# Gate/up weights: two of the seven low parts of a half step made by an accumulating DMA

## The chip, the cores and the metric

The kernel runs on one core of a Trainium2 chip. The metric is the device time of one execution in microseconds. Before the change two runs took 1078.86 and 1079.63 us; the median is 1079.24.

## What is computed

The reference is a decoder trunk of two layers on 512 tokens of width 1024, all in float32. Each layer is a mixer and a feed-forward part, each with an RMS norm before and after it and a residual sum. Layer 0 mixes with two kinds of attention, layer 1 with a causal pooling. The change touches the first half of the feed-forward part alone, the gate and up projections:

```
def swiglu(h, w_gate, w_up, w_down):
    return (jax.nn.silu(h @ w_gate) * (h @ w_up)) @ w_down
```

`w_gate` and `w_up` are 1024 x 2816, `w_down` is 2816 x 1024, one of each per layer.

## The kernel before

**Split operands.** TensorE multiplies float32 in a rounded form (the type fp32r in the rows). To keep the precision, every operand is kept as a high part (rounded to fp32r) and a low part (what the rounding left), and each product is three matmuls: high by high, high by low of the activations, and low by high (`three`, L325 to L328; L328 is the one that reads the weight's low part). For weights the parts are made by `conv` (L235 to L238): ScalarE copies the float32 operand into the fp32r tile `wh` (L237), and VectorE, for the gate/up weights, subtracts that copy from the operand into `wl` (L238; key `slo`). Each part is a tile of 128 x 512 float32, 256 KB.

**Half steps.** Gate and up are done by column pairs: 11 pairs of 2 x 128 columns per layer, for each pair first gate and then up, so 22 half steps per layer and 44 in all. A half step is one level of a Strassen-Winograd scheme with seven products of 256 columns, each 12 matmuls. Its weights are seven operands of four row blocks: '11', '22', 's1', 's3', '12', 's2', 's4', in the order in which `pair_weights` (L889 to L923) makes them. They come from two raw tiles `wr` of 512 KB, loaded by SP (L894); raw tile 0 holds blocks a11 and a12, raw tile 1 a21 and a22. The sums s1 to s4 are made in place in those tiles (`comb`, L904 to L906): s1 = a21 + a22 into a22 on VectorE, s3 = a11 - a21 into a21 on POOL, s2 = s1 - a11 into a11 on VectorE, s4 = a12 - s2 into a12 on POOL. So the 's4' sum overwrites a12, which is the operand of '12' before that, and it may only do so when both parts of '12' have been made from it.

**Short steps.** For three pairs of layer 0 and two of layer 1 the products with '11' and '12' are made ahead, while the norms of the layer are still running (`front`). Their half steps lack '11' and '12' and have five products. In each layer these pairs alternate with others until they are used up, so the first part of a gate/up stretch has full and short half steps in turn, and the rest has full ones alone.

**Products and banks.** `run` (L925 ff.) puts out, for half step i: `begin` with '11' (bank psA, operand uh) and '22' (psO, th), then `end` of step i-1 with 's4' (psS, uh), then `middle` with 's1' and 's3' (psS, th), '12' (psA, uh) and 's2' (psO, th). VectorE adds the products up from PSUM (L951 to L957 and L963), ScalarE does the silu (L967), POOL the product of gate and up (L977).

**Buffers and order.** All high and low parts of weights share ten tiles, the tag `wq`, five parts' worth; the raw tiles have four, the tag `wr`, two half steps' worth. A planner walks through the instructions with its own estimate of what each costs, takes for each engine the ready instruction of the highest priority, and fixes by that the order on every engine; `tc.high_priority` moves weight preparation to the front. On the chip each engine then runs its list in that order and waits at an instruction whose inputs or buffers are not ready. DMAs are issued by SP, a few by ScalarE, none by POOL.

Of the kernel before, what the change touches and what calls it, by code (L numbers as in the profile page):

```python
# [9 lines left out]
AF = mybir.ActivationFunctionType  # L10
ALU = mybir.AluOpType
AX = mybir.AxisListType

P = 128
# [15 lines left out]
CFG = dict(  # L30
    order=ORDER,
    norm='vggvgvvg',
    wlo0='g',
    wlo1='ggv',
    ng=31,
    no=8,
    xe=4,
    pt=4,
# [2 lines left out]
    jk=2,  # L41
    psb=(2, 2, 2, 2),
    early=('kc', 'vc'),
    hpe=50,
    hpw=0,
    wloe='g',
# [9 lines left out]
    slo='v',  # L56
# [56 lines left out]
def trunk(ctx: ExitStack, tc, x, norm_g, w_in, b_f, cmp_pe, cmp_w1, cmp_w2, w_out,  # L113
          pool_w, pool_scale, w_gate, w_up, w_down, cst_d, bands_d, out):
    nc = tc.nc
# [40 lines left out]
    def BANK(tag, shape=(P, S)):  # L156
        return ps.tile(list(shape), F32, tag=tag, bufs=psb[tag], name=nm(tag))

    def r32(ap):
        return ap.bitcast(F32)  # L160
# [4 lines left out]
    def cols(w, c0, n, k0=0, nk=KC):  # L165
        return w[k0 * P:(k0 + nk) * P, c0:c0 + n].rearrange("(k p) f -> p k f", p=P)

# [1 line left out]
    cst = cp.tile([P, C_END], F32, name="cst")  # L169
    ident = cst[:, C_ID:C_ID + P]  # L170
    strip_nsa = cst[:, C_NSA:C_NSA + S]
# [34 lines left out]
        nc.tensor.transpose(pp[:, 0:64], pe2, ident[0:64, 0:64])  # L206
        nc.scalar.activation(peTs, pp[:, 0:64], AF.Copy)

# [1 line left out]
    def split(dst_hi, dst_lo, src):  # L210
        nc.scalar.activation(dst_hi, src, AF.Copy)
        nc.vector.tensor_sub(dst_lo, src, r32(dst_hi))
# [7 lines left out]
    def load_w(src, shape, alloc=None):  # L220
        raw = T(shape, "wr", CFG["wr"])
        nc.sync.dma_start(raw, src)
        return split_w(raw, shape, alloc)
# [8 lines left out]
    def next_engine(key):  # L232
        return nc.vector if choose(key) == "v" else nc.gpsimd

    def conv(hi, lo, src, key="wlo"):  # L235
        with tc.high_priority(CFG["hpw"]):
            nc.scalar.activation(hi, src, AF.Copy)  # L237
            next_engine(key).tensor_tensor(lo, src, r32(hi), op=ALU.subtract)  # L238
# [59 lines left out]
        return T([P, KC, S], "uh", 1, F32R), T([P, KC, S], "ul", 1, F32R)  # L298

    def transpose_pair(dst, srcs, ks, tag, gcol=None):  # L300
        """dst(k) -> (hi, lo) of [128, 256]: the transposed column blocks ks of two token tiles"""
        pt = BANK(tag)
        for a, k in enumerate(ks):
            for j in range(2):
                nc.tensor.transpose(pt[:, a * 256 + j * P:a * 256 + (j + 1) * P], srcs[j][:, k * P:(k + 1) * P], ident)
        hi, lo = dst
        if gcol is None:
            split(hi, lo, pt.rearrange("p (k c) -> p k c", k=2))
            return
        for a, k in enumerate(ks):  # L310
            g = gT[:, gcol * 8 + k:gcol * 8 + k + 1]
            o = pt[:, a * 256:(a + 1) * 256]
            nc.scalar.activation(hi[:, a, :], o, AF.Copy, scale=g)
            nc.vector.scalar_tensor_tensor(lo[:, a, :], o, g, r32(hi[:, a, :]), op0=ALU.mult, op1=ALU.subtract)
# [20 lines left out]
            three(pa[:, 0:cs.stop - cs.start], wh[k], wl[k], uh[:, k, cs], ul[:, k, cs], k == 0, k == KC - 1)  # L335
        return pa

    # ================= layer 0: FoX || NSA =================
    w0 = w_in[0]
    early = [split_w(raw, [P, KC, P]) for raw in early_raw]  # L340
    u = alloc_u()
# [24 lines left out]

    env = {}

    # -- block compression --
    kcs = cp.tile([P, 2, 2, 32], F32R, name="kcs")  # L370
    kcA, kcB = kcs[:, :, 0, :], kcs[:, :, 1, :]
    nc.gpsimd.memset(r32(kcs), 0.0)
# [57 lines left out]
                        move(VCs[g][rows, r, 0:DH], tmp[0:NCB, g, DH:P])  # L430
                        move(VCs[g][rows, r, DH:P], tmp[0:NCB, g, 0:DH])

    # -- keys and queries, stacked along the contraction --
    def key_stack(name):
        pa = proj0(name)
        res = []
        with tc.high_priority(CFG["hpe"]):
            for g in range(2):
                q = slice(g * DH, (g + 1) * DH)
                o = slice((1 - g) * DH, (2 - g) * DH)  # L440
                kh, kl = (G([P, S], F32R, label=n_) for n_ in ("knh", "knl"))
                nc.scalar.activation(kh[q], pa[q, :], AF.Copy)
                nc.vector.tensor_sub(kl[q], pa[q, :], r32(kh[q]))
                move(kh[o], kh[q])
                move(kl[o], kl[q])
                res.append((kh, kl))
        return res
# [32 lines left out]
                    move(kB[DH + 2 + i:DH + 3 + i], env["cc"][i][h:h + 1])  # L480
                fx[h] = ((qA, kA), (qB[0:DH + 4], kB[0:DH + 4]))

    # -- values: [token, d] with high and low parts side by side --
    def v_load(pieces, groups, alloc):
        ws = []
        width = sum(n for _, n in pieces)
        k0 = 0
        for g_, nk in enumerate(groups):
            raw = T([P, nk, width], "wr", CFG["wr"])
            c = 0  # L490
            for c0, n in pieces:
                nc.sync.dma_start(raw[:, :, c:c + n], cols(w0, c0, n, k0, nk))
                c += n
            k0 += nk
            if alloc is None:
                his, los = split_w(raw, [P, nk, width])
            else:
                hi, lo = (alloc(g_, [P, nk, width], l_) for l_ in ("vwh", "vwl"))
                conv(hi, lo, raw)
                his, los = ([w_[:, k, :] for k in range(nk)] for w_ in (hi, lo))  # L500
            ws += list(zip(his, los))
        return ws
# [14 lines left out]
                with tc.high_priority(CFG["hpe"]):  # L517
                    put(per * tp + j, pa[:, j * width:(j + 1) * width])

    # -- forget gates and branch gates, projected beside the values of the NSA branches --  # L520
    def nsa_values():
        gt = cp.tile([P, NT, 32], F32, name="gates")

# [24 lines left out]
        nc.vector.scalar_tensor_tensor(cc[1], c, 8.0, r32(cc[0]), op0=ALU.mult, op1=ALU.subtract)  # L548
        env["gt"], env["cc"] = gt, cc

    # -- softmax and P^T for one (head, branch) and half of the queries --
    def softmax_unit(half, passes, strip, scale, gate):
        E = XE([P, 1024], label="E")
        its = (0, 1) if half == 0 else (2, 3)
# [209 lines left out]
            res.append(t_)  # L764
        return res

    # -- out[token, :] = sum over contraction chunks; the last chunks token tile by token tile --
    def down(get, nchunk, w, res):
        banks, acts = {}, {}

# [57 lines left out]
    class Ffn:  # L828
# [6 lines left out]
            self.g = bcast(norm_g[layer, 2], "g2", where)  # L835

        def weights(self, p):
            """the first column chunk of a pair, whose two products with the first half of the tokens run ahead"""
            self.ws[p] = [load_w(cols(w_[self.layer], 2 * p * P, P), [P, KC, P], pair_g if p < CFG["eg"] else None)
                          for w_ in (w_gate, w_up)]  # L840

# [20 lines left out]
            next_engine("mul").tensor_tensor(a[0][:, 0:256], a[0][:, 0:256], a[1][:, 0:256], op=ALU.mult)  # L862

        def combine(self):
            """T1 = B12 - B11, T2 = B22 - T1, T3 = B22 - B12, T4 = B21 - T2, each transposed and split"""
            lo_, hi_ = slice(0, S), slice(S, D)
            ts = [[], [], [], []]
            for j in range(2):
                a, b = self.uns[j], self.uns[2 + j]
                t1, t2, t3, t4 = (G([P, S], label="tt") for _ in range(4))  # L870
                for o, x0, x1 in ((t1, b[:, lo_], a[:, lo_]), (t3, b[:, hi_], b[:, lo_]),
                                  (t2, b[:, hi_], t1), (t4, a[:, hi_], t2)):
                    next_engine("sadd").tensor_tensor(o, x0, x1, op=ALU.subtract)
                for m, t_ in enumerate((t1, t2, t3, t4)):
                    ts[m].append(t_)
            self.T = {}
            for n_, m in enumerate((0, 2, 3, 1)):
                his, los = [], []
                for k2 in range(2):
                    hi, lo = (G([P, 2, 256], F32R, label=l_) for l_ in ("th", "tl"))  # L880
                    transpose_pair((hi, lo), ts[m], (2 * k2, 2 * k2 + 1), "psT")
                    his += [hi[:, k, :] for k in range(2)]
                    los += [lo[:, k, :] for k in range(2)]
                self.T[m + 1] = (his, los)
# [2 lines left out]
            return [[u_[:, 4 * j + k, t * 256:(t + 1) * 256] for k in range(4)] for u_ in self.u]  # L887

        def pair_weights(self, w_, p):  # L889
            """the blocks of two column chunks and the sums of a Strassen-Winograd step, high and low parts"""  # L890
            raws = []
            for a in range(2):
                raw = T([P, KC, P], "wr", CFG["wr"])
                nc.sync.dma_start(raw, cols(w_, (2 * p + a) * P, P))  # L894
                raws.append(raw)
            (a11, a12), (a21, a22) = ((r_[:, 0:4, :], r_[:, 4:8, :]) for r_ in raws)
            W = {}

            def put(name, src):
                hi, lo = WQ2([P, 4, P])  # L900
                conv(hi, lo, src, "slo")
                W[name] = ([hi[:, k, :] for k in range(4)], [lo[:, k, :] for k in range(4)])

            def comb(o, x0, x1, op):  # L904
                with tc.high_priority(CFG["hpw"]):
                    next_engine("sadd").tensor_tensor(o, x0, x1, op=op)  # L906

            if p not in self.ws:
                put("11", a11)
            put("22", a22)  # L910
            comb(a22, a21, a22, ALU.add)
            put("s1", a22)
            comb(a21, a11, a21, ALU.subtract)
            put("s3", a21)
            if p not in self.ws:
                put("12", a12)
            comb(a11, a22, a11, ALU.subtract)
            put("s2", a11)
            comb(a12, a12, a11, ALU.subtract)
            put("s4", a12)  # L920
            return W
# [127 lines left out]
    for step in CFG["tr1"].split():  # L1049
        steps[step[0]](*(int(c) for c in step[1:]))  # L1050

    # ================= layer 1: pooling mixer =================
    class Pool:
        def __init__(self):
            self.v = []
# [130 lines left out]
```

## Time and profile before

| | |
|---|---|
| two runs, median | 1078.86 and 1079.63 us, 1079.24 us |
| profiled execution: span, first to last instruction | 1076.4 us |
| the two runs above that span | 2.5 and 3.2 us |
| mean granted TensorE clock | 0.987 |
| gate/up of layer 0 | about 320 to 548 us |
| gate/up of layer 1 | about 720 to 950 us |

The profiled execution has no time of its own beside the span; the runs lie 2.5 to 3.2 us above it. A share of busy time on the page is a mean over the whole span, in which the stretches differ much; a group's mean duration covers the instruction alone and beside other engines; and the end of a matmul is modelled, so the distance from one matmul's start to the next says more than its length. A row's bracket names the idle time of the engine ahead of the instruction and who ended it.

### The profile page before, as it was taken

Reading aid. Unit: us, or ns where it says so; the run is one execution under the profiler, and the core shown is the slowest. Engines: PE = TensorE matmul, PEld = TensorE weight load, DVE = VectorE, ACT = ScalarE, POOL = GpSimd, SP = SyncE. Lnnn points to the kernel's source line nnn. Section 1 sums busy time; section 2 is a strip of 40 time slices with the busy share of each in tenths; the row PEclk is TensorE's granted clock in tenths of the full one; section 3 lists DMA queues with packets and bytes.
Section 4 is the critical chain, followed back from the end, with each engine's and each line's share of the span. In section 5 each row is a group of like instructions: output and inputs, shape, how many; then the busy total and the mean of one; then the engine's idle time right before and its main releaser. Section 6 shows DMA issues by size and latency. Waiting matters only on the chain.

```text
span 1076.4 us, 18708 instructions
## 1 busy us (share of the span) xinstructions
PE 1032.2 (96%) x6892; PEld 944.7 (88%) x6892; DVE 783.5 (73%) x1488; ACT 563.5 (52%) x1172; POOL 511.0 (47%) x421
## 2 busy tenths in 40 slices
PE   7999999999999999999999998989999999999997
PEld 6899888977899989899988886989889999988886
DVE  4449797767578999999991034788999999992123
ACT  5557797688465344444472234664444444472221
POOL 3815667666762444434454353362444334454340
PEclk9999999999999999999999999799999999999999
DMA  7920202233603333333334355003343343334222
GB/s 226 205 62 21 79 12 70 61 115 121 177 22 97 112 107 109 105 113 98 104 113 132 118 159 154 21 11 90 97 118 101 96 118 99 99 118 137 88 69 79
DMA packets 153419, 108.55 MB, mean 101 GB/s; under 512 B 11764, under 2 KB 134512, under 8 KB 153328
## 3 DMA queue, kind: packets, MB, share of 16 engines
q1 hardware_dynamic: 152528, 106.22, 33.7%
q8 instruction: 54, 0.88, 0.3%
q10 hardware_dynamic: 800, 1.15, 0.3%
q14 instruction: 37, 0.30, 0.1%
HBM read 101.88 MB, written 2.10 MB: 97 GB/s over the span
## 4 chain that ended last, share of the span: by engine, by line
PE 73%; DVE 15%; ACT 4%; issue 4%; DMA 2%; POOL 2%; DVEq 0%; POOLq 0%; ACTq 0%; SPq 0%
PE psA L328 5%; PE psA L326 5%; PE psA L327 5%; DVE wl L238 5%; PE psS L326 5%; PE psS L328 5%; PE psS L327 5%; PE psO L326 3%; PE psO L327 3%; PE psO L328 3%; PE psT L774 2%; PE psT L775 2%; PE psO L775 2%; PE psT L776 2%; PE psO L774 2%
## 5 line engine op out<-in xcount | busy, mean ns | idle before, releaser
L237 ACT ACTIVATE wh<-wr 128x512 fp32r<-128x512 f32 x420 | 252.8, 626 | 314.2 <-DVE wr L906 106.9
L238 DVE TENSOR_TENSOR wl<-wr,wh 128x512 fp32r<-128x512 f32 x318 | 297.0, 959 | 106.0 <-ACT wh L237 105.3
L238 POOL TENSOR_TENSOR wl<-wr,wh 128x512 fp32r<-128x512 f32 x102 | 144.4, 1426 | 137.7 <-ACT wh L237 128.6
L328 PE MATMUL psA<-uh,wl 128*128 128x256 f32 (+1 forms) x408 | 129.3, 317 | 0.5 <-DVE wl L238 0.5
L326 PE MATMUL psA<-uh,wh 128*128 128x256 f32 (+1 forms) x408 | 128.7, 315 | 0.4 <-ACT comb L940 0.4
L327 PE MATMUL psA<-ul,wh 128*128 128x256 f32 (+1 forms) x408 | 128.1, 314 | 0.0
L906 POOL TENSOR_TENSOR wr<-wr,wr 128x512 f32<-128x512 f32 x44 | 57.4, 1304 | 142.0 <-DVE wr L906 97.6
L906 POOL TENSOR_TENSOR wr<-wr 128x512 f32<-128x512 f32 x44 | 59.3, 1348 | 105.9 <-DVE wl L238 80.1
L326 PE MATMUL psS<-th,wh 128*128 128x256 f32 x352 | 100.9, 287 | 6.6 <-ACT wh L237 4.8
L328 PE MATMUL psS<-th,wl 128*128 128x256 f32 x352 | 101.4, 288 | 4.5 <-DVE wl L238 4.3
L327 PE MATMUL psS<-tl,wh 128*128 128x256 f32 x352 | 100.5, 286 | 0.0
L328 PE MATMUL psO<-th,wl 128*128 128x256 f32 x352 | 99.8, 284 | 0.6 <-DVE wl L238 0.6
L327 PE MATMUL psO<-tl,wh 128*128 128x256 f32 x352 | 99.8, 284 | 0.0
L326 PE MATMUL psO<-th,wh 128*128 128x256 f32 x352 | 99.5, 284 | 0.0
L328 PEld LDWEIGHTS psA<-uh,wl 128*128 128x128 f32 x408 | 78.3, 192 | 6.9 <-DVE wl L238 2.8
L326 PEld LDWEIGHTS psA<-uh,wh 128*128 128x128 f32 x408 | 78.2, 192 | 4.6 <-ACT comb L940 0.6
L327 PEld LDWEIGHTS psA<-ul,wh 128*128 128x128 f32 x408 | 78.3, 192 | 3.8
L977 POOL TENSOR_TENSOR act<-comb,comb 128x512 f32<-128x512 f32 (+1 forms) x44 | 71.9, 1649 | 11.6 <-DVE comb L963 6.2
L326 PEld LDWEIGHTS psS<-th,wh 128*128 128x128 f32 x352 | 67.7, 192 | 8.0 <-ACT wh L237 5.8
L328 PEld LDWEIGHTS psS<-th,wl 128*128 128x128 f32 x352 | 67.8, 193 | 6.8 <-DVE wl L238 6.7
L264 POOL TENSOR_SCALAR E<-E,ri 128x128 f32<-128x128 f32 (+3 forms) x48 | 54.6, 1139 | 40.0 <-DVE ri L582 16.7
L328 PEld LDWEIGHTS psO<-th,wl 128*128 128x128 f32 x352 | 67.4, 192 | 1.5 <-DVE wl L238 1.5
(343 smaller groups left out, 2972.2 us busy)
## 6 DMA issues: line engine op xcount, KB each, us to landing
wr<-in_ffn_w_gate_dram SPq DMA_DIRECT2D x49, 512.0 KB
wr<-in_ffn_w_up_dram SPq DMA_DIRECT2D x49, 512.0 KB
wr<-in_ffn_w_down_dram SPq DMA_DIRECT2D x44, 512.0 KB
wr<-in_attn_w_in_dram SPq DMA_DIRECT2D x20, 512.0 KB
wr<-in_attn_w_out_dram SPq DMA_DIRECT2D x8, 512.0 KB
x<-in_x_dram SPq DMA_DIRECT2D x4, 512.0 KB
gbc<-in_norm_g_dram SPq DMA_DIRECT2D x8, 256.0 KB
h<-in_x_dram SPq DMA_DIRECT2D x4, 512.0 KB
```

The source lines that it names most:

```text
L237: nc.scalar.activation(hi, src, AF.Copy)
L238: next_engine(key).tensor_tensor(lo, src, r32(hi), op=ALU.subtract)
L264: (nc.vector if k == "v" else nc.gpsimd).tensor_scalar(e, e, s1, None, op0=ALU.mult)
L326: nc.tensor.matmul(psum, wh, ah, start=first, stop=False)
L327: nc.tensor.matmul(psum, wh, al, start=False, stop=False)
L328: nc.tensor.matmul(psum, wl, ah, start=False, stop=last)
L774: nc.tensor.matmul(o, acts[c][0][:, tok], wh[k], start=first, stop=False)
L775: nc.tensor.matmul(o, acts[c][0][:, tok], wl[k], start=False, stop=False)
L776: nc.tensor.matmul(o, acts[c][1][:, tok], wh[k], start=False, stop=last)
L906: next_engine("sadd").tensor_tensor(o, x0, x1, op=op)
L977: next_engine("mul").tensor_tensor(a_, xg[:, rows, :], xu[:, rows, :], op=ALU.mult)
```

## The change

The low parts of '12' and 's4' are no longer made by ScalarE and a VectorE subtraction, but by ScalarE twice and a DMA that POOL issues: ScalarE writes the negated operand, rounded to fp32r, into the low tile, then the operand, rounded, into the high tile; then the DMA reads the float32 operand from the raw tile and adds it onto the low tile, which so holds operand minus high part. The other five parts are made as before. 

```
+    dlo=('12', 's4'),
...
             def put(name, src):
                 hi, lo = WQ2([P, 4, P])
-                conv(hi, lo, src, "slo")
+                if name in CFG["dlo"]:
+                    with tc.high_priority(CFG["hpw"]):
+                        nc.scalar.activation(lo, src, AF.Copy, scale=-1.0)
+                        nc.scalar.activation(hi, src, AF.Copy)
+                        nc.gpsimd.dma_start(r32(lo), src, accum_op=ALU.add)
+                else:
+                    conv(hi, lo, src, "slo")
                 W[name] = ([hi[:, k, :] for k in range(4)], [lo[:, k, :] for k in range(4)])
```

The other lines of the diff remove comments.

## Rows read from the trace of the kernel before

**Rows 1.** The page: engine, busy us (share of the span), instructions.

```profile
PE   1032.2 (96%) x6892; PEld 944.7 (88%) x6892; DVE 783.5 (73%) x1488; ACT 563.5 (52%) x1172; POOL 511.0 (47%) x421
```

**Rows 2.** Stretches: length, busy (count) PE PEld DVE ACT POOL, granted clock, DMA share, GB/s.

```profile
356.00:395.00 39.00, 36.35 (x288) 35.03 (x288) 37.24 (x61) 17.07 (x29) 17.12 (x13) 1.00 0.37 109
...
795.00:833.00 38.00, 37.27 (x294) 36.94 (x295) 35.14 (x57) 17.93 (x31) 15.00 (x12) 0.96 0.34 98
465.00:545.00 80.00, 79.99 (x654) 78.51 (x652) 76.34 (x122) 38.91 (x67) 34.36 (x25) 1.00 0.34 100
830.00:940.00 110.00, 109.99 (x897) 107.94 (x896) 105.65 (x170) 51.56 (x90) 47.64 (x34) 1.00 0.36 106
```

**Rows 3.** TensorE's two longest waits, 345 to 465 us: us in total, times, longest.

```profile
PE psS L326 <- ACT wh L237: 2.9, 3, 1.0
PE psS L328 <- DVE wl L238: 2.7, 5, 0.7
```

**Rows 4.** The same, 745 to 835 us.

```profile
PE psS L326 <- ACT wh L237: 1.9, 2, 1.0
PE psS L328 <- DVE wl L238: 1.7, 3, 0.7
```

**Rows 5.** Time line of a mixed stretch, VectorE and two matmuls: start, us, instruction [idle].

```profile
392.89 1.66 DVE L906 TENSOR_TENSOR wr<-wr 128x512 f32<-128x512 f32 x1
...
395.33 0.38 PE L326 MATMUL psS<-th,wh 128*128 128x256 f32 x1 [0.96 <-ACT wh L237]
...
396.57 0.39 PE L328 MATMUL psS<-th,wl 128*128 128x256 f32 x1 [0.74 <-DVE wl L238]
```

**Rows 6.** A stretch at the lower clock, columns as in rows 2.

```profile
397.50:400.90 3.40, 3.40 (x18) 3.40 (x17) 2.79 (x4) 1.26 (x2) 1.28 (x1) 0.50 0.02 5
```

**Rows 7.** Groups by line and shape: count | busy us, mean ns | idle before.

```profile
L238 DVE TENSOR_TENSOR wl<-wr,wh 128x512 fp32r<-128x512 f32 x318 | 297.0, 959 | 106.0 <-ACT wh L237 105.3
...
L951 DVE TENSOR_TENSOR comb<-psO,comb 128x256 f32<-128x256 f32 x34 | 14.2, 418 | 7.8 <-PE psO L328 7.8
...
L237 ACT ACTIVATE wh<-wr 128x512 fp32r<-128x512 f32 x420 | 252.8, 626 | 314.2 <-DVE wr L906 106.9 <-POOL wr L906 61.8 <-PE psO L775 54.3
...
L977 POOL TENSOR_TENSOR act<-comb,comb 128x512 f32<-128x512 f32 x39 | 65.9, 1708 | 11.6 <-DVE comb L963 6.2 <-DVE comb L955 4.2 <-ACT wh L237 1.2
```

**Rows 8.** Time line of one full half step: VectorE, ScalarE, POOL.

```profile
490.63 3.86 DVE L238 TENSOR_TENSOR wl<-wr,wh 128x512 fp32r<-128x512 f32 x3 [0.15 <-ACT wh L237]
...
494.74 0.68 DVE L906 TENSOR_TENSOR wr<-wr 128x512 f32<-128x512 f32 x1
...
498.25 1.28 DVE L238 TENSOR_TENSOR wl<-wr,wh 128x512 fp32r<-128x512 f32 x2
...
499.79 1.68 DVE L238 TENSOR_TENSOR wl<-wr,wh 128x512 fp32r<-128x512 f32 x1
501.62 1.89 DVE L238 TENSOR_TENSOR wl<-wr,wh 128x512 fp32r<-128x512 f32 x3 [0.15 <-ACT wh L237]
...
496.88 1.16 ACT L237 ACTIVATE wh<-wr 128x512 fp32r<-128x512 f32 x2 [0.45 <-POOL wr L906]
...
499.61 1.31 POOL L906 TENSOR_TENSOR wr<-wr 128x512 f32<-128x512 f32 x1 [2.76 <-DVE wl L238]
```

**Rows 9.** TensorE in that half step: '12' (two rows), then 's4'.

```profile
499.77 0.28 PE L326 MATMUL psA<-uh,wh 128*128 128x256 f32 x1
...
501.45 0.28 PE L328 MATMUL psA<-uh,wl 128*128 128x256 f32 x1
...
507.21 0.28 PE L328 MATMUL psS<-uh,wl 128*128 128x256 f32 x1
```

**Rows 10.** An SBUF to SBUF move: its issue; DMA busy tenths, 150.5 to 154.5.

```profile
151.26 0.50 SPq L163 DMA_DIRECT2D fqB<-fqA  x1
...
DMA  0000000000060000000598959431000000000000
```

**Rows 11.** SP's issues of the two weight loads of a half step: start, both together.

```profile
487.98 4.59 SPq L894 DMA_DIRECT2D wr<-in_ffn_w_gate_dram  x2
```

## The prediction

> **What bounds the kernel now.** I read the busy shares first, then the gate/up stretches alone, then who made TensorE wait there, then the time line of one step.
>
> The page gives TensorE 96% of the span and VectorE 73% [rows 1]. By stretch that mean falls apart: the stretches at 356 to 395 and 795 to 833 us, where steps with seven products and steps with five alternate, keep VectorE busy 37.2 of 39 and 35.1 of 38 us, and TensorE falls short of its stretch; at 465 to 545 and 830 to 940 all steps have seven products, and TensorE has no idle time at all, VectorE some 95% [rows 2]. So VectorE paces the mixed steps, TensorE the full ones. What TensorE waits for in the mixed steps are high and low weight parts: 5.6 us in layer 0 and 3.6 in layer 1 [rows 3, 4]. One such place is at 395.33, where the high part comes late behind a slow VectorE sum of 1.66 us [rows 5]. TensorE waits 0.96 us there and 0.74 at 396.57, and from 397.5 its granted clock is 0.50 (the 1.2 GHz level) for 3.4 us [rows 5, 6]; in layer 1 the stretch from 795 has a mean clock of 0.96, so one more such drop [rows 2].
>
> That is all this change can give back. At full clock 654 matmuls take 79.99 us, 0.122 each [rows 2]; the half-clock stretch holds 18, 2.2 us worth of work in 3.4, so 1.2 lost [rows 6], 2.4 for two. Bound of the gain: 5.6 + 3.6 + 2.4 = 11.6 us.
>
> **The change part by part.** There are 44 half steps: 34 have all seven parts, 10 have their first products made ahead and lack '11' and '12' (the first sum of the full steps is counted x34 [rows 7]). So '12' is made 34 times and 's4' 44 times.
>
> *Removed:* 78 VectorE subtractions at 0.959 us [rows 7], 75 us of an engine; per full step two. In a period of two full and two short steps, about the 39 us from 356 to 395, six go, 5.8 of the 37.2 us that VectorE works [rows 2]. The 1.9 us that TensorE waits per period (5.6 over three of them) are less than that.
>
> *Added on ScalarE:* 78 passes at 0.626 us [rows 7], 49 us. ScalarE works 38.9 of 80 us in full steps [rows 2], 4.9 in a step of 10.1; 1.25 more fits. The high part now comes second, so 0.63 later: the copies of 's3' and '12' end at 498.04, '12' would have its high part at 498.7, and its first matmul stands at 499.77 [rows 8, 9]. Nothing on the path, with 1.1 us of cover; if that goes, 0.6 per step.
>
> *Added on POOL:* 78 DMA issues. No POOL issue is in this trace. From below: SP's issue of an SBUF to SBUF move, 0.50 us [rows 10]; from above: POOL's longest common instruction, 1.71 [rows 7]. POOL works 34.4 of 80 us there [rows 2], 4.3 per step; two issues fit as work. Its order is the risk: at 499.61 it waited 2.76 us for the subtraction of '12' before it overwrites that operand with the 's4' sum [rows 8]. Now that sum waits until the DMA of '12' has landed, and behind the waiting sum stand the 's4' DMA, the next step's 's3' sum and, every second step, two products of 1.7 us.
>
> *Added on the DMA engines:* call F the time from the end of the negated copy to the landing of the sum. The nearest row is a move of 128 KB: issued at 151.26, moving in slices 19 to 27 of 0.1 us (152.4 to 153.25), so 1.1 us to the first packet and 0.85 to move [rows 10]. The new transfer is 256 KB. Low end, if adding runs like copying: 1.1 + 1.7 = 2.8. High end: 1.2 more for the issue (1.71 instead of 0.50) and twice the moving time because two operands are read: 2.3 + 3.4 = 5.7. I take 4.0: nearer the row's end for the move itself, with some for POOL's issue and for the weight loads, which fill a third of the engines' time [rows 2].
>
> *What F meets.* In the full step of rows 8 and 9, '12' has its copy at 498.04 and its low part is read at 501.45: lead 3.4. 's4': 498.04 + F, then the sum 1.31, the negated copy 0.63 and F again; its low part is read at 507.21. So 498.04 + 2F + 1.94 = 507.21, break-even at F = 3.6. VectorE gives lead back: the three subtractions from 490.63 (3.86 us) lose one, 1.2 us, ahead of the sum at 494.74 that starts each round [rows 8]. With that, '12' has 4.6 and 's4' breaks even at F = 4.2; 's4' decides. At my F = 4.0 both land in time; past 4.2 each full step is late by 2(F - 4.2). At F = 2.8 nothing is late, at 5.7 it is 3.0 per step, 102 us over 34 steps. The ten short steps have no DMA of '12'; I cost them nothing.
>
> *Moved:* the buffer of the step's first raw tile comes free when the DMA of 's4' has landed, some 507 us instead of the end of the third subtraction (501.62 + 1.89 = 503.5) [rows 8]. SP, which issues two loads per step, the second 4.2 us behind the first [rows 11], then issues the second one about 3.5 us later. Four buffers hold two steps, and no wait for a weight load stands in rows 3 and 4, so I cost it at nothing; if the load is late instead, it would show as a ScalarE wait for DMA at the head of a step, at most 3.5 us in a step.
>
> **The sum.** Of the 9.2 us of weight waits I take 7 (the chain from sum to copy to matmul stays, and POOL still slows VectorE), of the 2.4 of half clock 1.2: -8.2. For full steps in which POOL's order costs something now and then I put +2. Against the span of 1076.4 that makes 1070.2; the two runs lie 2.5 and 3.2 us above the span, the median 2.8. Forecast: 1079.2 - 8.2 + 2 = **1073 us**, its own range 1066 to 1078.
>
> **One rule against the change.** VectorE's two-operand instructions and POOL's do collide: two subtractions at 498.25 take 1.28 us without POOL, one at 499.79 takes 1.68 beside POOL's sum [rows 8]. If that same collision held up POOL's writing of a DMA's descriptors, each of the 78 issues would wait out a VectorE instruction, which is what rival C prices. The Trainium skill, "SBUF — State Buffer" (sections "SBUF: two separate sides" and "Who interferes with whom"), warns that a DMA issued from GpSimd is starved of descriptors while VectorE holds the shared port pair; but it gives the lock to copy, cast and tensor_scalar, and says that a two-input tensor_tensor contends only with a GpSimd instruction that reads SBUF. The collision in the rows named agrees with that last point; on descriptors no row here speaks. By the warning alone the sum would be rival C's, by the narrower statement mine stays.
>
> **The rivals.**
> - *A, the DMA lands too late (slower).* Place: the 's4' low part, behind POOL's sum that waits for the DMA of '12'. Price 2(F - 4.2) on 34 steps. For it: POOL's wait of 2.76 already, and the DMA takes the place of a 0.68 us instruction. Against it: one DMA per link, a clear lead, and an order that is planned anew. At F = 4.8: 1.2 us x 34 = 41, so 1079 - 8 + 41 = 1112. It is beyond 2% (1100.8) once it costs 30 us with the gain, 0.87 per step, F = 4.64. Chance 25% beyond 2%, and 15% for F between 4.2 and 4.6, 1078 to 1100.
> - *B, nothing gained.* The low parts are early but the waits pass to the weight buffers (ten tiles, five parts) or to the sum of 's1', as full steps are bound by TensorE anyway. Then the 8.2 shrinks to 0 and the small loss stays: 1078 to 1084. 11%.
> - *C, issues starved by VectorE.* F grows by about 1.0 (between 0.64 and 1.68 for one instruction), to 5.0 or so: 2 x 0.8 x 34 = 54, so 1125. 3%.
> - *The edit gives more than its bound,* since a new order also mends waits elsewhere, to below 1057.7: 1%.
> - The forecast: 45%.
>
> **How the numbers follow.** A measurement of this kernel can tell about 2% from no change. Faster by that needs 21.6 us, and the bound is 11.6: 1%. Slower: 25 + 3 = 28%. Within: 45 + 15 + 11 = 71%. Range 1065 to 1115: below lies 2%, above the upper half of A (13%) and C (3%).
>
> **What would show it.** Right: VectorE's subtraction group x240 instead of x318; its busy time in the mixed stretches down by about 5 us in 38; the waits of rows 3 and 4 mostly gone; TensorE without idle time in 465 to 545; POOL waiting for a DMA ahead of its 's4' sum without anyone waiting for POOL. Wrong by A: TensorE waits for DMA at the bank psA ('12') or at psS with the operand uh ('s4'), in every full step, and a DMA flight above 4.2 us from the negated copy; perhaps the clock falls behind each such wait. Wrong by B: VectorE eased but TensorE's matmuls in the mixed stretches still waiting for ScalarE copies. Wrong by C: POOL issues whose length follows VectorE's instructions.

## The result, and the profile after

The changed kernel takes 1212.97 us (two runs, 1212.76 to 1213.18) against 1079.24: ratio 1.124, 95% interval 1.122 to 1.126. It is 134 us slower. The forecast was 1073, the range ended at 1115; the direction belongs to rival A, the size to nothing that was priced.

Busy times of the whole execution, against [rows 1]:

```profile
PE 1086.0 (90%) x6892; PEld 978.4 (81%) x6892; DVE 724.4 (60%) x1410; ACT 602.5 (50%) x1250; POOL 574.2 (47%) x499
```

VectorE is eased by 59 us and TensorE is no longer kept busy. By stretch (columns as in [rows 2]). The first is still mixed, the second holds full half steps alone, and the third, since all work now lies later, has two short half steps up to about 865 us:

```profile
356.00:395.00 39.00, 34.57 (x265) 32.25 (x263) 28.91 (x48) 18.27 (x32) 20.30 (x17) 1.00 0.57 141
465.00:545.00 80.00, 69.04 (x503) 65.33 (x503) 45.98 (x84) 34.65 (x64) 31.90 (x29) 0.94 0.51 118
...
830.00:940.00 110.00, 90.28 (x651) 84.50 (x649) 67.98 (x114) 44.24 (x79) 47.21 (x41) 0.94 0.50 116
```

In 465 to 545 TensorE does 503 matmuls where it did 654, VectorE has work for 46 of 80 us, ScalarE for 35, POOL for 32. No engine is full, so a chain across them sets the pace. TensorE's waits in the two gate/up parts, layer 0 and then layer 1 (us in total, times, longest):

```profile
PE psS L327 <- ACT wh L905: 15.4, 15, 1.2
PE psA L329 <- DMA wl<-wr: 13.9, 10, 2.8
PE psS L329 <- DMA wl<-wr: 2.9, 2, 2.5
```

```profile
PE psA L329 <- DMA wl<-wr: 16.3, 17, 2.5
PE psS L327 <- ACT wh L905: 11.9, 10, 1.2
PE psS L329 <- DMA wl<-wr: 10.6, 10, 2.5
PE psA L327 <- ACT wh L238: 10.3, 6, 1.7
```

L904 is now the negated copy, L905 the copy, L906 the DMA, L913 the sums, and the matmul lines moved on by one. These seven rows are 81 us where [rows 3] and [rows 4] had 9.2. They lie at '12' (psA, low part, waiting for its DMA), at 's4' (psS with uh, its high part waiting for ScalarE more than its low part for the DMA) and, in layer 1 (the last row), at the high part of '11'.

The mean granted clock fell from 0.987 to 0.953 of full speed. Set against the spans that is (1 - 0.953) x 1211.4 = 57 us of clock given up where it was 14. 43 us more is an upper end for what the clock took, since part of it fell into idle time; the other run had a lower mean clock still, 0.943, and took no longer. With 78 us of waits for weights more (the seven rows and smaller ones: 88.1 against 9.8) this makes up 121 of the 135 us by which the span grew. The distances between the starts of the gate/up matmuls in the two traces give nearly all of it: those above 0.45 us, **pauses**, hold 93 us more than before, and those from 0.17 to 0.45 us, a slower **pace** than the usual 0.12, hold 38 us more. A pause comes out longer than the wait in a row, because the row counts from a matmul's modelled end.

One full half step shows the chain. Three timelines of it, POOL, ScalarE and VectorE (start in us, duration, instruction, [idle before it]):

```profile
544.41 0.87 POOL L906 DMA_DIRECT2D wl<-wr  x1 [1.49 <-PE psS L329]
...
550.03 1.29 POOL L913 TENSOR_TENSOR wr<-wr 128x512 f32<-128x512 f32 x1 [1.18 <-DMA wl<-wr]
552.28 0.89 POOL L906 DMA_DIRECT2D wl<-wr  x1 [0.96 <-ACT wl L904]
555.16 1.27 POOL L913 TENSOR_TENSOR wr<-wr,wr 128x512 f32<-128x512 f32 x1 [2.00 <-DVE wr L913]
```

```profile
543.50 0.62 ACT L904 ACTIVATE wl<-wr 128x512 fp32r<-128x512 f32 x1
...
551.35 0.63 ACT L904 ACTIVATE wl<-wr 128x512 fp32r<-128x512 f32 x1 [6.19 <-POOL wr L913]
551.88 0.61 ACT L905 ACTIVATE wh<-wr 128x512 fp32r<-128x512 f32 x1
552.40 1.14 ACT L238 ACTIVATE wh<-wr 128x512 fp32r<-128x512 f32 x2
555.19 0.63 ACT L238 ACTIVATE wh<-wr 128x512 fp32r<-128x512 f32 x1 [1.65 <-DVE wr L913]
...
557.36 0.62 ACT L904 ACTIVATE wl<-wr 128x512 fp32r<-128x512 f32 x1
```

```profile
553.05 1.29 DVE L239 TENSOR_TENSOR wl<-wr,wh 128x512 fp32r<-128x512 f32 x2 [0.87 <-ACT wh L238]
554.38 0.69 DVE L913 TENSOR_TENSOR wr<-wr 128x512 f32<-128x512 f32 x1
```

Read it as a circle. At 543.50 ScalarE makes the negated copy of '12'; at 544.41 POOL issues its DMA; at 550.03, when it has landed, POOL makes the 's4' sum over its operand; ScalarE, which sat idle for 6.19 us for that sum, makes both 's4' copies from 551.35, and only then, in its order, '11' and '22' of the next half step (552.40). VectorE subtracts for '11' and '22', makes the 's1' sum (554.38), POOL the 's3' sum (555.16), and at 557.36 ScalarE is at the next '12'. One **round** took 13.9 us, and TensorE's seven products take 84 x 0.12 = 10.1. In the kernel before the 's1' sums stand at 483.76, 494.74 [rows 8] and 504.39, so a round took 11.0 and 9.7 us in turn, 10.3 on average, with the 's4' sum 1.6 us behind the copy of '12' (498.04 to 499.61 [rows 8]). Now it is 5.9 us behind the negated copy (544.12 to 550.03).

This half step is not alone. ScalarE's copies for both parts, and POOL's 's4' sums, over the whole execution (columns as in [rows 7]):

```profile
L904 ACT ACTIVATE wl<-wr 128x512 fp32r<-128x512 f32 x78 | 48.9, 627 | 178.5 <-POOL wr L913 161.9 <-PE psA L329 12.5 <-PE psA L328 3.3
```

```profile
L913 POOL TENSOR_TENSOR wr<-wr 128x512 f32<-128x512 f32 x44 | 58.7, 1333 | 140.5 <-DMA wl<-wr 67.4
```

ScalarE stands 161.9 us behind POOL's sums, and POOL 67.4 us or more behind the DMA. In the full half steps of layer 0 a round took 13.4 to 14.0 us. In layer 1 short rounds of 12.5 to 13.4 alternate with long ones of 15.6 to 18.4; in the long ones ScalarE's copy of the bank psA (L947), which stands ahead of '12' in its order, waits 2.1 to 4.2 us for TensorE. So there TensorE is itself a part of the circle.

Why that long? The DMA's two landings of this half step and the one before, by two windows of the DMA view (issue count, KB, us from issue to landing; '12' from 543 to 551, 's4' from 538 to 543):

```profile
wr<-in_ffn_w_gate_dram SPq DMA_DIRECT2D x1, 512.0 KB
wl<-wr POOLq DMA_DIRECT2D x1, 256.0 KB, 5.5
```

```profile
wr<-in_ffn_w_up_dram SPq DMA_DIRECT2D x1, 512.0 KB
wl<-wr POOLq DMA_DIRECT2D x1, 256.0 KB, 3.3
```

The load in the first window is issued at 544.70, 0.3 us behind the DMA of '12', and moves beside it; the load issued at 542.15 moves after 543, when 's4' has landed. That '12' takes 2.2 us longer beside a load is seen; that the load is the reason is not proved by this. It holds for nearly all of them, though. Read DMA by DMA, 33 of the 34 flights of '12' have 128 KB or more of weight loads moving beside them, and '12' lands in 5.5 us in the median; 39 of the 44 flights of 's4' have next to none, and 's4' lands in 3.3.

### The profile page after: what moved, and what is told of

It reads as the page before. It is cut to its first block, busy times and chain, and to the rows that moved or that the text cites. A ratio compares the mean times of both kernels' runs of the same rounds, so it can differ in the third digit from the quotient of the medians.

```text
span 1211.4 us, 18950 instructions
## 1 busy us (share of the span) xinstructions
PE 1086.0 (90%) x6892; PEld 978.4 (81%) x6892; DVE 724.4 (60%) x1410; ACT 602.5 (50%) x1250; POOL 574.2 (47%) x499
## 3 DMA queue, kind: packets, MB, share of 16 engines
q1 hardware_dynamic: 152528, 106.22, 30.5%
q0 software_dynamic: 11232, 20.45, 10.0%
## 4 chain that ended last, share of the span: by engine, by line
PE 55%; DMA 15%; DVE 10%; ACT 7%; issue 6%; POOL 6%; SPq 0%; POOLq 0%; ACTq 0%; DVEq 0%
DMA wl<-wr 11%; PE psA L327 4%; PE psA L329 4%; PE psA L328 4%; PE psS L329 3%; PE psS L327 3%; PE psS L328 3%; POOL wr L913 3%; PE psO L327 2%; PE psT L775 2%; PE psT L777 2%; PE psO L777 2%; PE psT L776 2%; PE psO L775 2%; PE psO L776 2%
## 5 line engine op out<-in xcount | busy, mean ns | idle before, releaser
L238 ACT ACTIVATE wh<-wr 128x512 fp32r<-128x512 f32 x342 | 209.9, 626 | 217.4 <-PE psO L776 60.6
L239 DVE TENSOR_TENSOR wl<-wr,wh 128x512 fp32r<-128x512 f32 x240 | 213.1, 898 | 170.7 <-ACT wh L238 169.2
L329 PE MATMUL psA<-uh,wl 128*128 128x256 f32 (+1 forms) x408 | 135.0, 331 | 30.2 <-DMA wl<-wr 30.2
L327 PE MATMUL psA<-uh,wh 128*128 128x256 f32 (+1 forms) x408 | 136.1, 333 | 11.4 <-ACT wh L238 10.3
L904 ACT ACTIVATE wl<-wr 128x512 fp32r<-128x512 f32 x78 | 48.9, 627 | 178.5 <-POOL wr L913 161.9
L913 POOL TENSOR_TENSOR wr<-wr 128x512 f32<-128x512 f32 x44 | 58.7, 1333 | 140.5 <-DMA wl<-wr 67.4
L327 PE MATMUL psO<-th,wh 128*128 128x256 f32 x352 | 104.9, 299 | 0.3
L906 POOL DMA_DIRECT2D wl<-wr x78 | 68.7, 881 | 75.8 <-ACT wl L904 51.0
L913 POOL TENSOR_TENSOR wr<-wr,wr 128x512 f32<-128x512 f32 x44 | 57.2, 1300 | 89.0 <-DVE wr L913 89.0
L327 PE MATMUL psS<-uh,wh 128*128 128x256 f32 x200 | 64.8, 324 | 27.3 <-ACT wh L905 27.3
L328 PEld LDWEIGHTS psA<-ul,wh 128*128 128x128 f32 x408 | 82.9, 203 | 3.9
L329 PE MATMUL psS<-uh,wl 128*128 128x256 f32 x200 | 62.7, 313 | 13.9 <-DMA wl<-wr 13.5
```

The costliest lines, as they stand in the source:

```text
L327: nc.tensor.matmul(psum, wh, ah, start=first, stop=False)
L328: nc.tensor.matmul(psum, wh, al, start=False, stop=False)
L329: nc.tensor.matmul(psum, wl, ah, start=False, stop=last)
L904: nc.scalar.activation(lo, src, AF.Copy, scale=-1.0)
L906: nc.gpsimd.dma_start(r32(lo), src, accum_op=ALU.add)
```

## The experiments

Two theories stood against each other. **Round**: preparation is a circle through in-order engines, and a landing in series with it lengthens every half step. **Flight**: each DMA is late for its own product, wherever it stands. All kernels start from the changed one; ratios are to the kernel before. An edit lets the planner order the instructions anew, so each difference includes a new order; only in the plain-copy run is the order on every engine seen to be the same.

**Only 's4' by DMA.**

```
-    dlo=('12', 's4'),
+    dlo=('s4',),
```

> Only 's4' is made by the DMA (44 DMAs), '12' by the subtraction again. Theory (round): weight preparation runs in rounds on in-order engines, and the 's4' sum in place over the operand of '12' ties each round to the landing of the DMA of '12' (issue to landing up to 5.5 us where a subtraction took 1.3), so a round takes 13.5 us where TensorE's products take 10.1. Without that DMA the round is back at some 10.3 us: 1070 to 1090 us. Rival (flight): each DMA is late at its own product, 78 of them; 44 of 78 stay, so 44/78 of the 134 us: about 1155 us.

1114.72 us, 1.034 (1.032 to 1.037). 98 of the 134 us go, more than flight allows, fewer than the round theory said. No sum waits for a landing any more; what is left shows on ScalarE in that kernel:

```profile
500.62 0.63 ACT L904 ACTIVATE wl<-wr 128x512 fp32r<-128x512 f32 x1 [4.75 <-POOL wr L913]
501.15 0.61 ACT L905 ACTIVATE wh<-wr 128x512 fp32r<-128x512 f32 x1
501.67 1.14 ACT L238 ACTIVATE wh<-wr 128x512 fp32r<-128x512 f32 x2
```

The second pass of 's4' stands ahead of '11' and '22' of the next half step, and TensorE waits 1.39 us for the high part of '11' at 502.34; in the whole run it waits 14.1 us (12 times) for high parts at psA. So a pass alone, put into the circle, is paid too.

**Only '12' by DMA.**

```
-    dlo=('12', 's4'),
+    dlo=('12',),
```

> Only '12' is made by the DMA (34 DMAs), 's4' by the subtraction again. Theory (round): the round keeps the landing of '12' ahead of the 's4' sum; nearly all of the loss stays: 1180 to 1215 us. Rival (flight): 34 of 78 DMAs stay, 1138 us.

1195.35 us, 1.109 (1.108 to 1.111), inside the range of the round theory: 34 DMAs cost 116 of the 134 us, 44 others 36. Counting DMAs explains neither. Here the median landing is 5.2 us, in the run with 's4' alone 3.3.

**The 's4' sum over another operand.**

```
-            comb(a12, a12, a11, ALU.subtract)
-            put("s4", a12)
+            comb(a21, a12, a11, ALU.subtract)
+            put("s4", a21)
```

> Both DMAs stay, but the 's4' sum is written over a21 (the operand of 's3', long used) instead of over a12, so it no longer waits for the DMA of '12'. Theory (round): most of the 134 us go, 1070 to 1110 us; what stays is '12' landing late for its own product. Rival (flight): same number of DMAs and of issues, no change: 1200 to 1215 us.

1150.46 us, 1.067 (1.064 to 1.069), between both expectations. With all 78 DMAs in place 63 us go, and no row of POOL waiting for a DMA is left. So about half of the loss goes when the sum no longer waits. But '12' is still late for its own product: TensorE waits 29.0 us at psA for it, about what it was. That is not its flight, which is now 3.3 us in the median. 25 of the 29 us stand behind 13 DMAs that POOL issues over 1 us after the negated copy, mostly 3 to 4, because in its order two products come first. Here the copy had ended at 479.76:

```profile
479.57 3.35 POOL L984 TENSOR_TENSOR act<-comb,comb 128x512 f32<-128x512 f32 x2 [0.99 <-DVE comb L970]
482.87 0.87 POOL L906 DMA_DIRECT2D wl<-wr  x1
```

The long landing has gone over to 's4', 5.3 us in the median, whose flights now have the load beside them (33 of 44 with 128 KB or more). So it goes with the load, not with '12'; no run takes the load away, so its part is not separated.

**'s2' in place of '12'.**

```
-    dlo=('12', 's4'),
+    dlo=('s2', 's4'),
```

> Two parts by DMA as in the change, but 's2' in place of '12' (88 DMAs, all 44 half steps). Neither operand is overwritten by a later sum. Theory (round): no sum waits for a landing, 1070 to 1100 us. Rival (flight): ten DMAs more, 1210 to 1230 us.

1164.25 us, 1.079 (1.077 to 1.081). Both theories missed. No operand is overwritten, and yet TensorE waits 52.3 us for the low part of 's2', which is used soon after it is made: as I read it, a part with little lead is late by its landing. No run tests that alone.

**The addition by VectorE.**

```
-    nc.gpsimd.dma_start(r32(lo), src, accum_op=ALU.add)
+    nc.vector.tensor_tensor(lo, src, r32(lo), op=ALU.add)
```

> '12' and 's4' as in the change (negated copy, then copy, on ScalarE), but the addition is done by VectorE instead of the DMA; no DMA from POOL. Theory (round, sharpened by the run with 's4' alone): preparation is one chain through in-order ScalarE, VectorE and POOL per half step, with hardly any slack against TensorE's 10.1 us, so two passes of 0.63 us more in it cost some 0.5 to 1 us per step even without any landing: 1095 to 1125 us. Rival (flight): all of the loss is the DMA's landing, so with no DMA it is back at 1075 to 1085 us.

1108.45 us, 1.027 (1.025 to 1.029), as the round theory said. Without any DMA 29 us remain: the price of 78 second passes and of the order that the planner makes around them, which this run does not tell apart. I had costed both at nothing.

**A plain copy by the DMA.**

```
-    nc.gpsimd.dma_start(r32(lo), src, accum_op=ALU.add)
+    nc.gpsimd.dma_start(r32(lo), src)
```

> The DMA from POOL copies the operand over the negated copy instead of adding it (the addition is left out). Theory (round): what counts is the landing, 3.3 us and up to 7, of any DMA of this size beside the weight loads: 1200 to 1215 us. Rival (adding): adding two streams in the DMA engines makes the flight long; a plain copy lands over 1 us sooner and the time falls to 1150 us or below.

1136.96 us, 1.053 (1.052 to 1.055), and the rival was right: adding is what makes the flight long. This is the sharpest pair of the study, since all instructions stand in the same order on every engine as in the changed kernel. The DMA's row there and here (the issue view, median us to landing), the changed kernel and then this one, and this one's span and mean clock:

```profile
wl<-wr POOLq DMA_DIRECT2D x78, 256.0 KB, 3.6
```

```profile
wl<-wr POOLq DMA_DIRECT2D x78, 256.0 KB, 2.5
```

```profile
core 0: 1135.5 us, clock 0.985
```

Landings are 1.1 us sooner in the median of all 78, and the span is 76 us shorter. The landing that stands in the round is that of '12'. Matched one by one, its 34 landings are 2.2 us sooner on average (5.2 against 3.0, issue to landing), 75 us in sum; those of 's4' are 0.9 sooner. That is the round theory in numbers: one landing per full half step, nearly one for one. That 75 and 76 agree so closely is in part luck. The landings of 's4' got shorter too, and the 76 hold the clock: 17 us are given up instead of 57, so up to 40 are clock, and by the distances between matmuls 44 us are pauses and 33 pace. POOL's issue also shrank, from 0.88 to 0.56 us; that is a part of the shorter landings.

**'s4' put out behind '11' and '22' of the next half step**, by DMA and, as a control, by the subtraction. '12' is made by the subtraction in both, the control has `dlo=()`, and the 's4' of the last half step is put out after all other weights.

```
-    dlo=('12', 's4'),
+    dlo=('s4',),
...
             put("22", a22)
+            if self.late:
+                self.late()
...
-            put("s4", a12)
+            self.late = lambda: put("s4", a12)
```

> Only 's4' by DMA, and both its ScalarE passes and the DMA put out behind '11' and '22' of the next half step, in the order in which TensorE uses them. Theory (round): 's4' leaves the chain, since '11' and '22' no longer queue behind its two passes on ScalarE; against 's4' by DMA in its old place (1115 us) most of the 36 us go: 1075 to 1095 us. Rival (flight): 's4' lands later still against its product, two products after '22': over 1115 us.

> The same new place of 's4', made by the subtraction; no DMA at all. Theory (round): the chain of the kernel before gets shorter by one copy, so the mixed half steps wait less: 1066 to 1079 us. Rival: VectorE paces the mixed steps by its work alone, whatever the order: 1077 to 1082 us.

By DMA 1092.38 us, 1.014 (1.010 to 1.019), inside the range of the round theory: 22 of the 36 us of 's4' go by place alone. In this trace ScalarE waits 58.4 us (27 times) for gate and up loads, where the changed kernel has 12.3 (5 times). A late 's4' holds its raw tile longer, which is the likeliest reason for the 13 us that stay. By the subtraction 1081.13, 1.002 (1.001 to 1.003): the place in itself brings nothing to the kernel before, and its rival held.

**Weight loads in long rows.**

```
-    nc.sync.dma_start(raw, cols(w_, (2 * p + a) * P, P))
+    k = (2 * p + a) % KC
+    nc.sync.dma_start(raw.rearrange("p k f -> p (k f)"), w_[k * P:(k + 1) * P, 0:KC * P])
```

> The change, with weight loads of the same 512 KB that read other columns: one contiguous row of 4 KB per partition instead of eight pieces of 512 bytes (so the weights are not the right ones). Theory (round, with the landing of '12' lengthened by the weight load beside it, 5.5 us against 3.3 alone): the load is off the DMA engines sooner, '12' lands in 4 to 4.5 us and the time falls by 25 to 60 us, to 1150 to 1190. Rival: the length of a landing beside a load is POOL's or the queue's own, no change, 1200 to 1215 us.

1221.09 us, 1.132 (1.130 to 1.134). It does not decide: the loads have half as many packets but keep the DMA engines as long (queue share 30.3% against 30.5%), so the load beside '12' was not made shorter. The median landing is 3.7 us.

**'12' right behind '22'.** Same passes, DMAs and sums, one line moved.

```
             put("22", a22)
+            if p not in self.ws:
+                put("12", a12)
...
-            if p not in self.ws:
-                put("12", a12)
```

> The change with one thing moved: '12' is made right behind '22' instead of behind 's3'. Same passes, same 78 DMAs, same sum over a12. Theory (round): the landing of '12' runs beside the copies and sums of 's1' and 's3', some 4 us of the round, instead of in series with them, so the round loses most of the 5.5 us that the landing adds: 1100 to 1140 us. Rival (flight): each DMA costs what it costs, wherever it stands: 1195 to 1215 us.

1089.30 us, 1.010 (1.006 to 1.014), less than the round theory's 1100 to 1140: the place of one part gives back 124 of the 134 us. The landings have gone beside the work for 's1' and 's3'. They are little shorter: the median of all is 4.0 us, that of '12' falls from 5.5 to 4.2 and that of 's4' rises from 3.3 to 3.7. The 34 landings of '12' are 29 us shorter in sum, so at one for one, which is an estimate, 29 of the 124 us are flight, and the rest is place. POOL's and TensorE's waits for the DMA in that kernel, where the changed one had 67.4, 30.2 and 13.5 us:

```profile
POOL wr L913 <- DMA wl<-wr: 16.2, 7, 3.3
...
PE psA L329 <- DMA wl<-wr: 7.6, 6, 2.8
...
PE psS L329 <- DMA wl<-wr: 2.6, 2, 1.6
```

**Everything together**: '12' behind '22', the 's4' sum over a21, 's4' behind the next '22'.

> Both DMAs, with every landing taken out of the round: '12' is made right behind '22' (two products more ahead of its use), the 's4' sum is written over a21, and 's4' is made behind '11' and '22' of the next half step. Theory (round): the landings have 5 us and more of lead, what stays is the extra ScalarE passes, while VectorE has 75 us less: 1070 to 1095 us. Rival (flight and buffers): the parts hold their tiles longer, of which there are ten, and TensorE waits for DMA or copies again: over 1110 us.

1099.57 us, 1.019 (1.017 to 1.021): between both expectations, and worse than moving '12' alone. Which of the two other moves costs the 10 us was not tried. The trace points at the weight loads: ScalarE waits 103.6 us for gate and up loads where it waits 13.8 with '12' early alone, and no sum waits for a landing any more.

```profile
ACT wh L238 <- DMA wr<-in_ffn_w_up_dram: 58.5, 19, 6.4
ACT wh L238 <- DMA wr<-in_ffn_w_gate_dram: 45.1, 18, 4.1
```

**'12' early by DMA, 's4' by the subtraction.** '12' is moved behind '22' by the same lines as above.

```
-    dlo=('12', 's4'),
+    dlo=('12',),
```

> Only '12' by DMA, made right behind '22'; 's4' by the subtraction as before the change. Theory (round): no landing in series and no second pass of 's4' ahead of the next '11' and '22'; what stays is one pass of ScalarE per full step, in a place with cover, and VectorE has 34 subtractions (33 us) less: 1066 to 1084 us. Rival: any part made by two passes and a DMA costs the round its pass, some 0.3 us a step: 1085 to 1100 us.

1077.55 us, 0.999 (0.998 to 1.000): no version beats the kernel before by anything that counts. 34 subtractions less, some 33 us of VectorE's work, bring 1.3 us, which is not clear of nothing. The round theory's range, 1066 to 1084, holds it.

## Why the prediction was wrong

*What bounds the kernel now.* The rows were read rightly, and the bound of the gain held: the best version gives back at most some 1.3 of the 11.6 us. But "VectorE paces the mixed steps" was half a reading. VectorE was where the circle spent most of its time; in the full steps the round, at 10.3 us, lay just on TensorE's 10.1. A round that keeps TensorE full shows TensorE's own pace, so the kernel before does not tell how much slack the preparation had. I did not ask. The addition on VectorE tells: two more passes of 0.63 us cost 29 us, 0.85 for each of the 34 full half steps, so there was little.

*Removed.* Right: 240 subtractions remain, VectorE's time fell by 59 us, less than the 75, in part because other instructions became longer (the 's2' sum by 0.28 us on average).

*Added on ScalarE: "nothing on the path".* Wrong. I gave the second pass of '12' cover against its own product, 1.1 us, and never asked who stands behind it on ScalarE. Behind the second pass of 's4' stand '11' and '22', the head of the next round. The addition on VectorE prices this at 29 us in all.

*Added on the DMA engines: F = 4.0.* The median is about right: 3.6 us from issue to landing and some 0.3 ahead of it. But it mixes two kinds. 's4' lands in 3.3 in the median; '12', which decides, in 5.5, and up to 7.1, above my high end. For the doubled reading I had allowed 1.7 us; the pair with the plain copy shows about 1.0 without a load beside it (3.3 against 2.3) and 2.2 on average for '12', which flies beside one. The weight loads were named and given no term of their own.

*What F meets.* This step failed most. I took the two reads by TensorE as fixed dates, counted F twice against them, and charged only the overhang beyond 4.2. By that formula F = 5.8 for '12' (lead 4.6) and 3.6 for 's4' gives 1.2 us late at '12' and 1.0 at 's4', at most 41 us over 34 steps, where 134 were measured. In truth there is little lead to use up in a circle: by the pair with the plain copy each us of the landing of '12' cost its half step about one us, the slower pace behind the waits included. TensorE's half step is not a date, it starts when the round delivers. POOL's order, which I priced at 2 us as a risk, was where the sum stood that closed the circle; the 's4' sum over another operand alone gave 63 us back.

*Clock.* Rival A priced none of it beyond "perhaps". TensorE waited 1.23 us at 549.94 and 1.16 at 552.55, and from 552.6 its granted clock is 0.50 (columns as in [rows 2]):

```profile
552.60:556.00 3.40, 3.40 (x15) 3.36 (x16) 2.13 (x4) 1.57 (x3) 1.40 (x2) 0.50 0.44 77
```

15 matmuls in 3.4 us instead of 28. In the prediction the clock stood only among the gains.

*Rival C* is refuted. An issue takes POOL 0.87 us at the least, 0.88 in the median and 1.05 at most, while VectorE's instructions take 0.68 to 1.7: it waits for none of them. The Trainium skill, "SBUF — State Buffer" (section "Who interferes with whom"), says that tensor_tensor has no 2-port mode and with two inputs contends only with a GpSimd instruction that reads SBUF; these issue lengths agree.

*The moved load* was rightly costed at nothing: TensorE and ScalarE do not wait for gate/up loads in the stretches above, and over the whole execution ScalarE waits 12.3 us for them where it was 10.9. Where 's4' is put out late ScalarE does wait, as I had said it would show: 58.4 and 103.6 us in two of the runs above.

## What to carry to other kernels

Before a step is given to a slower path, follow it round until you come back to the same instruction of the next iteration: if the round is as long as the bound engine's work, nearly every us added in series is paid in every iteration, whatever the share of busy time says. Place a long-latency step as early in the round as its inputs allow, and see what overwrites its source, what stands ahead of its issue and which transfers it will fly beside; here that one place was worth 124 of 134 us. Then add the clock to the price of every new wait of a bound TensorE.

## What was not expected of the hardware

- An accumulating DMA of 128 x 512 float32 within SBUF lands 3.3 us after POOL begins its issue when no load moves beside it, a plain copy of the same size 2.3. For '12', which mostly has a weight load beside it, the medians are 5.5 and 2.8. POOL is busy 0.88 and 0.56 us for the two issues. The Trainium skill, "DMA: Bandwidth & Descriptors" (section "Anatomy of one DMA — SWDGE (gpsimd) path"), fits 2.0 us plus bytes over 436 GB/s. For 256 KB this is an estimate of 2.6 us; the plain copy's median of 2.5 agrees, the accumulating one does not.
- The software queue took 10.0% of the DMA engines' time for the additions and 5.3% for the copies, for the same 20.45 MB counted: 144 packets for each addition, 80 for each copy.
